# Convolved columns moved into a stage of seven-product multiplications, the SSD recurrence read by chunk from DRAM

## The chip, the cores and the metric

One core of a Trainium2 chip runs the whole kernel. TensorE (PE in the profile, with its weight loads as PEld) multiplies matrices, VectorE (DVE), ScalarE (ACT) and GpSimd (POOL) do the elementwise work, and every DMA of this kernel is issued from SyncE's queue (SP). The metric is the time of one execution on the device in microseconds (us). The kernel before took 2466.53 us, the median of three runs (2464.01 to 2472.35).

## What is computed

One layer of a hybrid recurrent decoder, on 1072 tokens in one pass: 16 learned meta tokens, 8 sample sequences of 4 tokens and a prompt of 1024 tokens. Each of the three kinds has its own recurrent state. Cut to what matters:

```python
u = x @ w_in                 # 1024 -> 10280 columns
qk_pre, v, o_pre, i_pre, f_pre, z, xbc_pre, dt_pre, gate_pre = split_cols(u, IN_SPLITS)
qk = silu(causal_dwconv(qk_pre))              # 1024 columns, convolution over 4 tokens
h  = mlstm_chunked(q, k, v, ig, lf, mstate)   # 4 heads, chunks of 128 tokens
ya = (sigmoid(o_pre) * headnorm(h)) @ w_proj_a
xbc = silu(causal_dwconv(xbc_pre))            # 3072 columns: xs 2048, B 512, C 512
y  = ssd_chunked(xs, dt, Bm, Cm, A, S) + D * xs   # 32 heads in 4 groups, chunks of 128
yb = groupRMS(y * silu(z)) @ w_proj_b
g  = sigmoid(gate_pre)
x1 = layer_norm(ALPHA * x + (g[0] * ya + g[1] * yb) @ w_out)
upc = causal_dwconv(x1 @ w_up)                # 1024 -> 5632, convolution over 3 tokens
x2 = layer_norm(ALPHA * x1 + (silu(upc_a) * upc_b) @ w_down)
```

Both recurrences carry a state from chunk to chunk. The outputs are x2 and the new states of both recurrences and of the convolutions.

## The kernel before, in words

Activations lie with channels on the 128 partitions and tokens along the row. All products are in fp32r with both operands split into a high and a low part (`split`, L156 to L159: ACT makes the high part, DVE the low one), and each product is three matmuls, high by high, high by low and low by high (`mm3`, L173 to L175). A **block** is 128 output columns of a weight matrix of 1024 rows: 8 parts of the contraction, three stretches of about 357 tokens (or 353, where the first 14 tokens are not needed), three matmuls each, so 72 matmuls. `w_in` has 72 such blocks beside v and the small gates: 8 for q and k, 8 for o, 16 for z, 16 for xs, 8 for B and C, 16 for the merge gates.

`seven` (L213 to L296) multiplies two blocks at a time with seven half-size products in place of eight: the weights of a pair and the activations are cut into halves by halves, sums of quarters are formed, and 7 products of 4 parts, two stretches of 266 and 264 tokens and three matmuls give 168 matmuls for a pair. The sums of weights are made by POOL, split by ACT and DVE, five products ahead (`AHEAD`); the results are put together by DVE, ACT and POOL in `evac`. PSUM has 8 banks (`pg` 3, `pr` 5), and `seven` uses all of them in every pair.

The stages, in order:

1. Layer norm of x, v and the small gates (to about 169 us). At its end the forms of x for `seven` are made (`make_forms`) and 2 gate blocks run in full.
2. **Early stage**, `seven` on 12 pairs of w_in: o and z. o goes to DRAM as tanh (`od`), z as silu (`zd`).
3. **mLSTM stage**: four heads of nine chunks. Each head's q and k are multiplied in full (`conv_steps`: 72 matmuls, then the copy out of PSUM, three DVE operations over 1096 elements for the taps, a tanh and three DVE operations for silu). Behind head h come 2, 1, 1 and 2 blocks of xs, B and C of SSD group 0 (`FILLS`), stored to `xsd`. The result h goes to DRAM (`hd`).
4. **SSD stage**: four groups of eight heads, nine chunks each. `begin(c)` loads the decays of a chunk (`dec`, 8 rows of 128 tokens broadcast to 128 partitions, and `E`), applies mask and exp, transposes xs and B, and multiplies by C; `end(c)` forms the output, updates the state S and adds it into `xs` in place. xs, B and C of a whole group lie in SBUF. `weave` puts between these steps the blocks of xs, B and C of the next group, and gate blocks, and `z_steps` multiplies whole rows of the previous group by z, stores `yd` and sums squares.
5. 4 more gate blocks, then proj a (8 blocks on the eight pairs of `hd`), proj b (16 blocks), w_out (8 blocks) with the layer norm, and 4 blocks of w_up in full (1310 to 1763 us).
6. `seven` on 20 pairs of w_up with the convolution over 3 tokens beside it (`act_steps`), to about 2183 us, then w_down and the last norm.

The order of instructions on each engine is made ahead of the run by a list scheduler: it takes instructions by priority (the order in which they are written, moved forward inside `tc.high_priority`), when its own estimates say that their inputs are there and a buffer of their pool is free. On the chip each engine, and the SP queue, runs its list in that order and waits where something is late. Weights are loaded 150 priority steps ahead (`WAHEAD`).

Of the kernel before, what the change touches and what calls it, by code (L numbers as in the profile page):

```python
# [1 line left out]

# [10 lines left out]
ALU = mybir.AluOpType  # L13
# [23 lines left out]
HP = [(0, 266), (266, 264)]  # L37

PLAIN = 2

# [3 lines left out]


GATES = (2, 0, 2, 2, 2, 4, 4)

FILLS = (2, 1, 1, 2)
# [8 lines left out]
def kernel(ctx, tc, I, O):  # L57
# [9 lines left out]
    rc_cm = tc.tile_pool(name="rc", bufs=1, side="right")  # L67
# [9 lines left out]
    xd = dr.tile([KD, 128, TC], F32, name="xd")  # L77
# [6 lines left out]
    zd = dr.tile([16, 128, TC], F32, name="zd")  # L84
    xsd = dr.tile([6, 128, T], F32, name="xsd")
# [117 lines left out]
    def make_forms(src, dst):  # L203
# [5 lines left out]
        V.tensor_tensor(b21, b22, b21, ALU.subtract)  # L209
# [4 lines left out]
    def seven(pairs, raws, sums, X, tmp, xforms, evac, begin=None, between=None):  # L214
# [6 lines left out]
        wf = [wp.tile([128, 2, 4, 128], F32R, tag=t, name="wf") for t in ("wl", "ws", "wh") for _ in range(2)]  # L221
# [32 lines left out]
        X = X[:, 0:4 * 266].rearrange("p (a t) -> p a t", t=266)  # L254
        for n in range(AHEAD):
            prepare(n)
        for i in range(len(pairs)):
            if begin:
                begin(i)
            for p, xf in enumerate(xforms):  # L260
# [6 lines left out]
                for j, (t0, w_) in enumerate(HP):  # L267
# [52 lines left out]
    xh = xp.tile([128, KD, CUT + 2 * HC], F32R, name="xh")  # L320
    xl = xp.tile([128, KD, CUT + 2 * HC], F32R, name="xl")
    zero = rc.tile([128, KD, 2], F32, name="zero")
    V.memset(zero, 0.0)
    split(xh[:, :, T:], xl[:, :, T:], zero)
# [10 lines left out]
    with ExitStack() as c0:  # L335
# [13 lines left out]
        def norm_in(c, t0, n):  # L349
# [21 lines left out]
            o = CUT if c == 0 else 0  # L371
            dma(xd[:, :, t0 + o - CUT:t0 + n - CUT].rearrange("k p t -> p k t"), xf[:, :, o:n])
# [186 lines left out]
    ev = tc.tile_pool(name="ev", bufs=3, side="right")  # L559
# [27 lines left out]
    def conv_steps(pool, m, cw, st_in, st_out, alloc):  # L587

        w = win_load(m)
        u = pool.tile([128, 1100], F32, tag="u", name="u", bufs=2)  # L590
        si = pool.tile([128, NB, 3], F32, tag="si", name="si", bufs=2)
        dma(si, st_in.rearrange("p (b r) -> p b r", r=3))
        G.tensor_copy(win7(u)[:, :, 0:3], si)
        G.memset(u[:, 56:59], 0.0)

        def evac(j, t0, n, ps):
            if j == 0:
                S.copy(u[:, 59:75], ps[:, 0:NMETA])
                S.copy(win7(u)[:, :, 3:7], smp(ps[:, NMETA:NA]))
                S.copy(u[:, 75:27 + n], ps[:, NA:n])  # L600
            else:
                S.copy(u[:, 27 + t0:27 + t0 + n], ps)
        for j, _ in enumerate(gemm_steps(w, NT, x_rhs, evac)):
            if j < 2:
                yield
        so = pool.tile([128, 27], F32, tag="so", name="so", bufs=2)
        G.tensor_copy(so[:, 0:3], u[:, 1096:1099])
        G.tensor_copy(so[:, 3:27].rearrange("p (b r) -> p b r", r=3), win7(u)[:, :, 4:7])
        dma(st_out, so)
        cv = pool.tile([128, 1096], F32, tag="cv", name="cv")  # L610
        S.activation(cv, u[:, 0:1096], AF.Identity, scale=cw[:, 0:1], bias=cw[:, 4:5])  # L611
        for j in range(1, 4):
            V.scalar_tensor_tensor(cv, u[:, j:j + 1096], cw[:, j:j + 1], cv, op0=ALU.mult, op1=ALU.add)  # L613
        t = u[:, 0:1096]
        S.activation(t, cv, AF.Tanh)
        dst = alloc()
# [960 lines left out]
```

## Time and profile before

| | |
|---|---|
| median of 3 runs | 2466.53 us |
| profiled execution, whole | 2476.02 us |
| its span from first to last instruction | 2474.1 us |
| PE, PEld busy | 95%, 90% of the span |
| DVE, ACT, POOL busy | 68%, 39%, 27% |
| mean granted clock of TensorE | 0.978 |
| DMA | 310.6 MB, 126 GB/s on average |

The profile is one execution. A matmul's busy time overlaps the next one's, so the pace of TensorE is read from the number of matmuls in a stretch and not from the mean length of one. A stretch's count (x...) takes in the one or two instructions that are under way at its edges. DMA share is the mean busy share of the 16 DMA engines.

### The profile page before, as it was taken

The page shows a single profiled execution, that of the slowest core. Times are in us where ns is not written, and L with a number is a line of the kernel's source. Part 1 is how long each engine was busy: PE and PEld are TensorE (multiplying, and loading weights), DVE is VectorE, ACT ScalarE, POOL GpSimd, SP SyncE. Part 2 cuts the span into 40 slices and gives each one's busy share as a digit, 9 for nine tenths or more (in the row PEclk, how much of TensorE's full clock was granted, in tenths as well). Part 3 has the DMA queues.
Part 4 walks back from the last instruction along what each step waited for, and adds up shares of the span by engine and source line. Part 5 has one row for each costly group of instructions (what it writes and reads, how often), then busy time and mean ns, then how long its engine had stood idle before and what let it go on. Part 6 is the DMA issues. An engine that isn't in the chain of part 4 may idle for free. (4 is left out here: it accounts for less than half of the span.)

```text
span 2474.1 us, 40641 instructions
## 1 busy us (share of the span) xinstructions
PE 2356.4 (95%) x15603; PEld 2233.5 (90%) x15603; DVE 1675.8 (68%) x2871; ACT 972.8 (39%) x1996; POOL 662.9 (27%) x695
## 2 busy tenths in 40 slices
PE   7989999999999999898889999999899999999996
PEld 5879999898878888797789999999899999999996
DVE  7674455678758678785746557577988888874338
ACT  6234443444345445554522112245544444441111
POOL 0034331111024233332300000033655555510004
PEclk9989999999999999999989999999999999999998
DMA  8143332544354454635646433254222222282121
GB/s 244 51 147 112 103 104 87 162 152 143 126 176 129 144 152 102 207 84 181 156 157 239 140 104 122 77 162 148 90 80 80 80 80 80 89 271 80 46 65 70
DMA packets 191122, 310.62 MB, mean 126 GB/s; under 512 B 41080, under 2 KB 131032, under 8 KB 190928
## 3 DMA queue, kind: packets, MB, share of 16 engines
q1 hardware_dynamic: 190928, 308.03, 39.8%
q8 instruction: 122, 2.00, 0.3%
q14 instruction: 72, 0.59, 0.1%
HBM read 225.39 MB, written 82.58 MB: 124 GB/s over the span
## 5 line engine op out<-in xcount | busy, mean ns | idle before, releaser
L173 PE MATMUL gps<-xh,whi 128*128 128x358 f32 (+5 forms) x1176 | 404.7, 344 | 12.6 <-ACT evt L583 6.3
L175 PE MATMUL gps<-xh,wlo 128*128 128x358 f32 (+5 forms) x1176 | 393.9, 335 | 0.0
L174 PE MATMUL gps<-xl,whi 128*128 128x358 f32 (+5 forms) x1176 | 391.5, 333 | 0.0
L158 ACT ACTIVATE whi<-wst 128x1024 fp32r<-128x1024 f32 (+1 forms) x137 | 139.5, 1019 | 433.0 <-PE gps L174 261.8
L173 PEld LDWEIGHTS gps<-xh,whi 128*128 128x128 f32 (+1 forms) x1176 | 226.6, 193 | 27.2 <-issue 9.7
L159 DVE TENSOR_TENSOR wlo<-wst,whi 128x1024 fp32r<-128x1024 f32 (+1 forms) x137 | 170.2, 1244 | 105.6 <-ACT whi L158 105.5
L174 PEld LDWEIGHTS gps<-xl,whi 128*128 128x128 f32 (+1 forms) x1176 | 226.3, 192 | 10.9 <-issue 10.3
L175 PEld LDWEIGHTS gps<-xh,wlo 128*128 128x128 f32 (+1 forms) x1176 | 226.7, 193 | 5.2 <-issue 4.7
L173 PE MATMUL gps<-ph,whi 128*128 128x352 f32 (+1 forms) x472 | 155.1, 330 | 4.8 <-ACT whi L158 1.7
L175 PE MATMUL gps<-ph,wlo 128*128 128x352 f32 (+1 forms) x472 | 154.7, 328 | 0.3 <-DVE wlo L159 0.2
L174 PE MATMUL gps<-pl,whi 128*128 128x352 f32 (+1 forms) x472 | 154.8, 328 | 0.0
L274 PE MATMUL rps<-x1h,wf 128*128 128x266 f32 (+1 forms) x480 | 137.8, 287 | 1.7 <-ACT mix L279 1.7
L275 PE MATMUL rps<-x1l,wf 128*128 128x266 f32 (+1 forms) x480 | 137.7, 287 | 0.0
L889 ACT ACTIVATE dec<-dec,tk 128x128 f32<-128x128 f32 (+1 forms) x288 | 88.4, 383 | 124.2 <-POOL dec L886 112.7
L276 PE MATMUL rps<-x1h,wf 128*128 128x266 f32 (+1 forms) x480 | 137.1, 286 | 0.0
L159 DVE TENSOR_TENSOR wf<-raw,wf 128x512 fp32r<-128x512 f32 x96 | 105.1, 1096 | 32.8 <-ACT wf L158 31.5
L1288 DVE SCALAR_TENSOR_TENSOR mix<-mix,c_fcw 128x1072 f32<-128x1072 f32 x80 | 115.6, 1445 | 6.8 <-ACT mix L1286 6.7
L613 DVE SCALAR_TENSOR_TENSOR cv<-u,c_scw,cv 128x1096 f32<-128x1096 f32 x72 | 103.1, 1432 | 17.1 <-ACT cv L611 16.7
L173 PE MATMUL gps<-ah,whi 128*128 128x352 f32 x312 | 101.0, 324 | 0.0
L175 PE MATMUL gps<-ah,wlo 128*128 128x352 f32 x312 | 100.9, 323 | 0.0
L174 PE MATMUL gps<-al,whi 128*128 128x352 f32 x312 | 100.7, 323 | 0.0
L173 PE MATMUL rps<-ph,whi 128*128 128x352 f32 (+1 forms) x296 | 96.3, 325 | 0.0
(488 smaller groups left out, 7066.1 us busy)
## 6 DMA issues: line engine op xcount, KB each, us to landing
wst<-in_win SPq DMA_DIRECT2D x48, 512.0 KB, 4.4
raw<-in_wup SPq DMA_DIRECT2D x40, 512.0 KB, 3.6
dec<-btd SPq DMA_DIRECT2D x32, 512.0 KB, 5.9
gt<-gd SPq DMA_DIRECT2D x24, 529.0 KB, 3.5
raw<-in_win SPq DMA_DIRECT2D x24, 512.0 KB, 3.4
wst<-in_wout SPq DMA_DIRECT2D x24, 512.0 KB, 3.5
fd<-mix SPq DMA_DIRECT2D x22, 528.0 KB, 2.7
raw<-fd SPq DMA_DIRECT2D x22, 528.0 KB, 4.4
```

The costliest lines, as they stand in the source:

```text
L158: S.activation(hi, src, AF.Copy)
L159: V.tensor_tensor(lo, src, hi.bitcast(F32), ALU.subtract)
L173: PE.matmul(out, ah, bh, start=start, stop=False)
L174: PE.matmul(out, ah, bl, start=False, stop=False)
L175: PE.matmul(out, al, bh, start=False, stop=stop)
L274: PE.matmul(ps, wh[:, k], a, start=new and k == 0, stop=False, **chk)
L275: PE.matmul(ps, wh[:, k], b, start=False, stop=False, **chk)
L276: PE.matmul(ps, wl[:, k], a, start=False, stop=k == 3, **chk)
L613: V.scalar_tensor_tensor(cv, u[:, j:j + 1096], cw[:, j:j + 1], cv, op0=ALU.mult, op1=ALU.add)
L889: S.activation(dec[:n, i, 0:n], dec[:n, i, 0:n], AF.Exp, bias=tk2[:n, c, g * 8 + i:g * 8 + i + 1], scale=1.0)
L1288: V.scalar_tensor_tensor(cv, u[:, j:j + 1072], fcw[:, m, j:j + 1], cv, op0=ALU.mult, op1=ALU.add)
```

## The change

**`seven` takes all convolved columns.** The early stage becomes 28 pairs: 16 pairs of q, k, xs, B and C (`conv`) and 12 of o and z (`plain`), dealt so that one or two `conv` pairs stand before each `plain` one. The halves become 536 tokens (`HX`, stretches of 268 and 268) so that all 1072 tokens are there. The results of a `conv` pair are put into `uA` and `uB`; the taps, tanh and silu (`conv_steps`) run between the products of this pair and the next, and q and k go to `qkd`, xs, B and C to `xsd`, in DRAM. The fourth form of x has no tiles of its own any more: it overwrites the second half of `xh` and `xl` (k 0 to 3) and those are restored from `xd` behind the stage. The six tiles for split weights are taken in another order of pool tags.

```diff
-GATES = (2, 0, 2, 2, 2, 4, 4)
-FILLS = (2, 1, 1, 2)
+GATES = (2, (2, 2, 1, 1), 8)
+PROJ = 6
+RAHEAD = 60
...
-        wf = [wp.tile([128, 2, 4, 128], F32R, tag=t, name="wf") for t in ("wl", "ws", "wh") for _ in range(2)]
+        wf = [wp.tile([128, 2, 4, 128], F32R, tag=t, name="wf") for t in ("ws", "ws", "wh", "wl", "wh", "wl")]
...
+        for q in range(12):
+            to = 16 * (q + 1) // 12
+            for i in range(nc_, to):
+                jobs.append(conv[2 * i:2 * i + 2])
+            nc_ = to
+            jobs.append(plain[2 * q:2 * q + 2])
...
+        def conv_steps(b, to, cw, st_out):
+            u = us[b]
...
+            S.activation(cv, u[:, 0:1096], AF.Identity, scale=cw[:, 0:1], bias=cw[:, 4:5])
+            for j in range(1, 4):
+                V.scalar_tensor_tensor(cv, u[:, j:j + 1096], cw[:, j:j + 1], cv, op0=ALU.mult, op1=ALU.add)
+                yield
+            t = u[:, 0:1096]
+            S.activation(t, cv, AF.Tanh)
+            yield
...
+            dma(to, dst)
+            yield
...
+        run(state[0])
+        for k in range(4):
+            dma(last(k), xd[k, :, HX:T])
+            split(xh[:, k, HX:T], xl[:, k, HX:T], last(k))
```

**The mLSTM stage** loads q and k of a head from `qkd`, and behind the heads come 2, 2, 1 and 1 gate blocks.

```diff
-            for _ in range(FILLS[h]):
-                fill_unit(next(fills))
+            for _ in range(GATES[1][h]):
+                run(gate_steps(next(gates)))
             if h < 3:
-                qk = qk_units(h + 1)
+                qk = qk_load(h + 1)
```

**The SSD stage** keeps no group in SBUF. Each chunk loads its xs, B and C (`xc`, 6 x 128 rows of 512 bytes) and its z (4 x 128 rows), multiplies by z, stores `yd` (4 x 128 rows) and sums squares itself. Loads of `xc` and `dec` stand two chunks ahead (`open_`), the four groups are chained, and their steps have a priority of 60 (`RAHEAD`). `dec` has 3 buffers instead of 2, `xc` 4, `z`, `E`, `tmp` 2.

```diff
+            def open_(c):
+                t0, n = CHUNKS[c]
+                xc = stile([128, 6, 128], "xc", 4)
+                dma(xc, xsd[g, :, :, t0:t0 + 128].rearrange("i p t -> p i t"))
+                dec = stile([128, 8, 128], "dec", 3)
                 dma(dec[:n, :, 0:n], btd[g * 8:(g + 1) * 8, t0:t0 + n].partition_broadcast(n))
...
+            def begin(c):
...
+                zt = stile([128, 4, 128], "z", 2)
+                dma(zt[:, :, 0:n], zd[4 * g:4 * g + 4, :, t0:t0 + n].rearrange("i p t -> p i t"))
...
+                V.tensor_tensor(x, x, tmp[:, :, 0:n], ALU.add)
+                V.tensor_tensor(x, x, zt[:, :, 0:n], ALU.mult)
+                a = CUT if c == 0 else 0
+                dma(yd[4 * g:4 * g + 4, :, t0 + a - CUT:t0 + n - CUT].rearrange("i p t -> p i t"), x[:, :, a:n])
+                sq = tmp[:, :, 0:n]
+                S.activation(sq, x, AF.Square)
+                G.tensor_tensor(sq[:, 0:2], sq[:, 0:2], sq[:, 2:4], ALU.add)
```

**Proj a begins beside the SSD.** What is woven between the steps is now 8 gate blocks and then 6 of the 8 blocks of proj a; the pairs of `hd` are loaded and split there (`hpair`). The last two blocks of proj a are queued behind the last norm of the SSD.

```diff
+        def work():
+            for q in range(GATES[2]):
+                yield from gate_steps(next(gates))
+                if 2 <= q < 6:
+                    hpair(hq, hst, q - 2)
...
+            for k in range(4, 8):
+                hpair(pm, hst, k)
+            yield from chain(*proj)
+
+        weave(chained(0, 1, 2, 3), work(), 3 * (GATES[2] + PROJ))
...
+    yp = [ypair(k, pb) for k in range(2)]
+    for s_ in proj:
+        with tc.issue_after(held[-1].ins):
+            run(s_)
```

The pools of the later stages are laid out anew (`pm` 16, `pb` 12 and `pa` 12 buffers for `pa` 20 and `pb` 20).

## Rows read from the trace of the kernel before

**Rows 1.** The page: span, and busy time with its share of the span for each engine.

```profile
span 2474.1 us, 40641 instructions
PE 2356.4 (95%) x15603; PEld 2233.5 (90%) x15603; DVE 1675.8 (68%) x2871; ACT 972.8 (39%) x1996; POOL 662.9 (27%) x695
```

**Rows 2.** Busy time of each engine by stretch, one row a stage: early stage, mLSTM, SSD with the last gate blocks, proj to w_up in full, `seven` on w_up, w_down. Columns: stretch, its length, PE, PEld, DVE, ACT, POOL busy us (instructions), granted clock, DMA share, GB/s.

```profile
176.80:425.50 248.70, 248.37 (x1989) 247.63 (x1990) 132.31 (x240) 100.23 (x225) 85.14 (x71) 0.99 0.31 101
425.50:712.00 286.50, 283.16 (x1641) 256.24 (x1640) 211.01 (x532) 119.48 (x268) 36.39 (x74) 0.99 0.46 150
712.00:1310.00 598.00, 551.11 (x3543) 491.25 (x3542) 423.10 (x647) 282.21 (x736) 186.21 (x201) 0.95 0.52 148
1310.00:1763.00 453.00, 439.18 (x2677) 433.09 (x2676) 289.09 (x417) 135.99 (x191) 69.10 (x63) 0.99 0.42 137
1763.00:2183.00 420.00, 415.63 (x3348) 414.87 (x3347) 351.01 (x482) 202.34 (x368) 238.09 (x238) 0.99 0.27 89
2183.00:2474.10 291.10, 267.79 (x1676) 265.87 (x1674) 150.92 (x295) 55.63 (x63) 34.87 (x25) 0.97 0.30 98
```

**Rows 3.** The same view for stretches in which TensorE does one kind of work and is never idle: `seven` on w_up, `seven` on w_in, blocks with stretches of 352 or 354 tokens, blocks with 358 or 356.

```profile
1800.00:2150.00 350.00, 350.00 (x2850) 350.00 (x2850) 291.32 (x409) 166.61 (x305) 205.53 (x204) 1.00 0.24 80
250.00:300.00 50.00, 50.00 (x408) 50.00 (x407) 24.80 (x48) 20.43 (x45) 16.49 (x14) 1.00 0.29 95
1350.00:1400.00 50.00, 50.00 (x309) 50.00 (x308) 26.57 (x29) 9.58 (x9) 0.00 (x0) 1.00 0.51 159
430.00:460.00 30.00, 30.00 (x184) 30.00 (x184) 16.76 (x19) 13.25 (x33) 7.68 (x15) 1.00 0.76 246
```

**Rows 4.** The same view for line L173 alone (the first of the three matmuls of a product in full blocks): the counts tell how many blocks a stretch holds. Columns: PE, PEld busy (instructions), clock, DMA share, GB/s.

```profile
425.50:712.00 286.50, 124.72 (x375) 71.02 (x376) 0.99 0.46 150
712.00:1310.00 598.00, 256.26 (x728) 142.60 (x729) 0.95 0.52 148
```

**Rows 5.** What TensorE waited for, between 145 and 425 us.

```profile
PE rps L274 <- ACT wf L158: 7.1, 1, 7.1
```

**Rows 6.** DVE by line and form: in the mLSTM and SSD stages the taps, the writing out of a convolved block (three pieces), the splitting of a block's weights and the operations of a chunk; in the early stage the splitting of weights and two of the results; in `seven` on w_up the splitting of weights.

```profile
L613 DVE SCALAR_TENSOR_TENSOR cv<-u,c_scw,cv 128x1096 f32<-128x1096 f32 x72 | 103.1, 1432 | 17.1 <-ACT cv L611 16.7
...
L618 DVE SCALAR_TENSOR_TENSOR xs<-u,cv 128x1024 f32<-128x1024 f32 x12 | 16.4, 1364 | 0.0
...
L619 DVE SCALAR_TENSOR_TENSOR xs<-u,cv 128x32 f32<-128x32 f32 x12 | 6.5, 544 | 0.0
...
L618 DVE SCALAR_TENSOR_TENSOR xs<-u,cv 128x16 f32<-128x16 f32 x12 | 4.5, 372 | 5.7 <-ACT u L615 5.6
...
L159 DVE TENSOR_TENSOR wf<-sum,wf 128x512 fp32r<-128x512 f32 x48 | 38.1, 799 | 21.1 <-ACT wf L158 20.6
L159 DVE TENSOR_TENSOR wf<-raw,wf 128x512 fp32r<-128x512 f32 x36 | 32.0, 891 | 31.9 <-ACT wf L158 30.6 <-DMA raw<-in_win 1.3
...
L654 DVE TENSOR_TENSOR e<-rps,u 128x266 f32<-128x266 f32 (+1 forms) x24 | 10.3, 433 | 6.2 <-PE rps L276 5.9
...
L159 DVE TENSOR_TENSOR wf<-raw,wf 128x512 fp32r<-128x512 f32 x52 | 64.8, 1246 | 0.0
L159 DVE TENSOR_TENSOR wf<-mix,wf 128x512 fp32r<-128x512 f32 x68 | 47.0, 691 | 41.2 <-ACT wf L158 39.4
```

**Rows 7.** The DMA queue of all loads and stores, first in the mLSTM stage (425.5 to 712 us), then in the SSD stage (712 to 1310 us). Columns: packets, MB, share of 16 engines over the stretch.

```profile
q1 hardware_dynamic: 19640, 42.58, 45.2%
...
q1 hardware_dynamic: 85840, 88.09, 51.6%
```

**Rows 8.** Busy time by stretch again, for three stretches with much DMA: the first loads and stores of x, and two of the SSD stage. The last two columns are DMA share and GB/s.

```profile
15.00:60.00 45.00, 41.34 (x192) 31.09 (x192) 33.36 (x112) 31.92 (x72) 0.00 (x0) 1.00 0.95 238
1160.00:1185.00 25.00, 23.78 (x158) 19.08 (x159) 18.53 (x32) 10.58 (x29) 12.55 (x10) 1.00 0.81 259
1200.00:1225.00 25.00, 20.89 (x163) 16.03 (x161) 19.56 (x30) 13.30 (x46) 10.60 (x10) 1.00 0.61 125
```

**Rows 9.** DMA issues: operands, queue, count, KB of each, median us from issue to landing.

```profile
dec<-btd SPq DMA_DIRECT2D x32, 512.0 KB, 5.9
...
E<-ebtd SPq DMA_DIRECT2D x64, 128.0 KB, 4.8
...
va<-vd SPq DMA_DIRECT2D x4, 1024.0 KB, 7.1
...
qp<-wind SPq DMA_DIRECT2D x4, 536.0 KB, 5.4
```

**Rows 10.** What the SP queue waited for before it issued, in the SSD stage, longest first: line of the DMA, releaser, us in total, times, longest.

```profile
SPq L584 <- ACT evt L583: 106.7, 29, 7.7
SPq L609 <- POOL so L607: 49.7, 16, 8.9
SPq L592 <- POOL u L594: 47.6, 8, 8.4
SPq L877 <- PE rps L968: 40.9, 16, 6.5
```

More of the change, by code (lines that the diff above doesn't have):

```diff
@@ new lines @@
+        sx = [(M_XS + m, xsd[m // 4, m % 4] if m < 16 else xsd[m % 4, 4 + (m - 16) // 4],
+               scw[:, m], I["scs"][m], O["sco"][m]) for m in range(24)]
+        conv = qk + sx
+        plain = [(M_O + m, od[m], None) for m in range(8)] + [(M_Z + m, zd[m], True) for m in range(16)]
+        jobs, nc_ = [], 0
+        for q in range(12):
[4 more added lines that the diff above has]
+            jobs.append(plain[2 * q:2 * q + 2])
@@ new lines, in evac, with between @@
+            S.activation(e, c, AF.Tanh, scale=0.5)
+            if z:
+                V.scalar_tensor_tensor(e, e, 1.0, c, op0=ALU.add, op1=ALU.mult)
+                dma(job[1][:, t0:t0 + n], e)
+            else:
+                a0 = max(t0, CUT)
+                dma(job[1][:, a0 - CUT:t0 + n - CUT], e[:, a0 - t0:n])
+        state = [iter(())]
+        def between(i, p):
+            if is_conv[i] and p == 2:
+                run(state[0])
+                for b in range(2):
+                    x_begin(b, jobs[i][b][3])
+                return
+            if is_conv[i] and p == 4:
+                state[0] = conv_steps(0, *jobs[i][0][1:3], jobs[i][0][4])
+            if is_conv[i] and p == 6:
+                state[0] = chain(state[0], conv_steps(1, *jobs[i][1][1:3], jobs[i][1][4]))
+            near = is_conv[i] and is_conv[i + (1 if p > 3 else -1)]
+            for _ in range(2 if near else 1):
+                next(state[0], None)
@@ L683 @@
+        run(state[0])
+        for k in range(4):
+            dma(last(k), xd[k, :, HX:T])
+            split(xh[:, k, HX:T], xl[:, k, HX:T], last(k))
     with ExitStack() as c1:
@@ L1086, with weave @@
-    for m in gates:
-        run(gate_steps(m))
-    def ptile(dt, nm, w=TC, pool=pa):
-        return pool.tile([128, PW], dt, tag="P", name=nm)[:, 0:w]
-    def pair(src):
-        f = ptile(F32, "pf")
-        dma(f, src)
-        return pair_of(f)
-    def pair_of(f, pool=pa):
+                    steps.append(lambda c=c: ahead(c))
+                steps.append(lambda c=c: end(c))
+            return steps + [norm]
+        def weave(rec, work, n):
+            done = 0
+            for k, step in enumerate(rec):
+                with tc.high_priority(RAHEAD):
+                    step()
+                to = n * (k + 1) // len(rec)
+                for _ in range(to - done):
+                    next(work, None)
+                done = to
+            run(work)
@@ L1174 @@
         gemms(unit_b, prhs(yp))
-    mpair = [pair_of(mix[k]) for k in range(8)]
+    mpair = [pair_of(mix[k], pm if k < 4 else pa) for k in range(8)]
     summed = []
```

504 lines of the change are left out of this document (237 added, 267 removed).

## The prediction

> **What bounds the kernel now.** I read the busy times first [rows 1], then the same by stage [rows 2], then the pace of TensorE where it does one thing only [rows 3]. The reader should see that PE is at 95% and that no other engine has over 68%. By stage PE is full in the early stage and in `seven` on w_up, and loses time in the SSD stage: 551.1 of 598 us busy, granted clock 0.95, so a part of that stage also ran at the lower of the clock's two levels. So the end is set by TensorE: its matmuls, and what it loses beside the recurrences.
>
> Pace [rows 3], counts less 1.5 for the instructions at the edges: `seven` with about 265 tokens needs 350 us / 2848 = 122.9 ns a matmul, on w_in 123.0; full blocks 162.6 ns with 353 tokens and 164.4 ns with 357. The pace falls with the tokens, by (164.4 - 122.9) / 92 = 0.45 ns a token, so a product of fewer columns does cost less, and the slower pace per column eats part of it. A pair of blocks in full is 144 x 164.4 ns = 23.7 us; as seven products 168 x 122.9 ns = 20.65 us.
>
> **The change, part by part.** The sum is made on the profiled span of 2474.1 us.
>
> *Early stage.* With 268 tokens a matmul needs 122.9 + 3 x 0.45 = 124.2 ns, a pair 20.87 us, 28 pairs 584.4 us, against 248.7 now [rows 2]: **+335.7**. Taking 32 blocks out of the other stages removes 32 x 72 x 164.4 ns = 378.8 us, so the products alone give some 43 us.
>
> This holds if DVE keeps up. A `conv` pair costs it [rows 6] six tap operations x 1.432 = 8.6 us, two writings out x (1.364 + 0.372 + 0.544) = 4.6, seven splits of weights x 0.835 (70.1 / 84) to 0.93 (111.8 / 120) = 5.8 to 6.5, eight results x 0.43 = 3.4 and small pieces, about 0.6: 23 to 23.7 us, more than the 20.9 of PE. A `plain` pair costs 132.3 / 12 = 11 us [rows 2]. Over the stage that is 16 x 23.3 + 12 x 11 = 505 of 584 us (86%); over two `conv` pairs and a `plain` one 57.6 of 62.6 (92%). In `seven` on w_up DVE stands at 291 of 350 us (83%) and PE has no gap [rows 3]. Weights are split five products (15 us) ahead, and the taps may run into the next pair, so I expect the bursts to be absorbed but for a few us. Bounds: 0, and 3.5 x 16 = 56 us if nothing is absorbed (2.4 us of excess a pair, and splits at the 1.246 us of the slowest row would add 2.2 more: the middle). Restoring `xh` adds four splits behind the last product; they lie beside the first head's small matmuls, else cost some 4 us. Together I take **+6**.
>
> The stage now begins with 7.1 us in which PE waits for the first split weights [rows 5], because the tile was still held by the gate blocks. The new order of tags frees it earlier. Bounds 0 and -7, taken **-5**: what is late then is the load of the weights, which reuse the tiles in which the forms of x are made.
>
> *mLSTM stage.* It holds 375 / 24 = 15.6 blocks [rows 4], 185 us; the recurrence's own part is 286.5 - 185 = 101.6 us, 98.3 of it busy. After: six gate blocks x 72 x 162.6 ns = 70.3, plus the own part: 169 to 172 us if the blocks still fill each wait. They fill less, two behind a head or one (11.7 us) where there were three or four. At the start of a head `va` and `qp` need 7.1 and 5.4 us to land [rows 9], and both have a single buffer. Uncovered in every head that is some 9 x 4 = 36 us, so the bounds are 168 and 214. I take 178, near the row: **-108.5**. The q and k loads replace weight loads and cost nothing while DMA stays at half share [rows 2].
>
> *SSD stage.* It holds 728 / 24 = 30.3 blocks [rows 4], 358 us, and its own part is 240 us, 193 of it busy. After: eight gate blocks and six of proj a, 164 us. PE alone therefore asks for 357 us (no wait left) to 404 us (the same waits as now).
>
> The new term is DMA. From the two stages [rows 7] a price follows for packets and bytes: 45.2% of 286.5 is 129.5 us for 19,640 packets and 42.58 MB; 51.6% of 598 is 308.6 us for 85,840 and 88.09. Solved: 0.90 us a thousand packets and 2.63 us a MB, all 16 engines together. A full chunk moves rows of 512 bytes: `xc` 768, `dec` 1024, `E` 512, `z` 512, `yd` 512, together 3328 packets and 1.70 MB, where it moved 1536 of that kind. 32 full chunks, four short ones (10,700 packets, 2.9 MB), the sample states in and out (16.8 MB), 14 weights (7.3), gates and `hd` (12), and the 4-byte packets of the semaphores: about 136,000 packets and 94.5 MB, so 123 + 248 = **371 us** of all 16 engines. In the stretch from 15 to 60 us [rows 8] a share of 0.95 was held for 45 us, so a stage of 390 us is possible, and it lies within what PE asks for. DVE (5.6 us a chunk, some 280 with the rest) and ACT stay below. I take 390: **-208**. Bounds: 357, if PE alone decides, and 464 (below).
>
> The Trainium skill, "DMA: Bandwidth & Descriptors", section Specifications, gives 512 bytes as the least size that moves at line rate. The price from the rows disagrees: 0.90 + 0.512 x 2.63 = 2.25 us a thousand packets of 512 bytes, 40% of which goes with the packet and not with its bytes. By the rule only the bytes would count, 94.5 x 2.63 = 248 us, DMA would be no limit, and the third rival would come out.
>
> *Proj a.* Six of eight blocks leave the stage after 1310 us: **-70.3** (they are counted above). The last two wait in order behind the last norm of the SSD; their 23 us cover the loads of the first pairs of y. Smaller pools further on can hold an act of w_down until the last product on w_up is done, 2 us at most; costed at nothing.
>
> *Sum.* 2474.1 + 335.7 + 6 - 5 - 108.5 - 208 - 70.3 = 2424 us. Outside the span lie 1.9 us (2476.02 - 2474.1), so 2426. The profiled execution is 1.0038 times the median of the three runs, so the median should be **2417 us**, 2% less.
>
> **The rivals.**
>
> *DMA starves the SSD stage (slower).* All transfers go through one SP queue, which waits in order. A store of `yd` waits for the multiplication by z, and a load of `dec` or `E` for a buffer; everything written behind them waits too, the weights of proj a among them. SP already waits 106.7 us at the stores of gates and 40.9 us at `dec` [rows 10]. Against it: loads stand two chunks ahead. In the SSD stage the share was 0.81 and 0.61 in two stretches that move the most [rows 8]. At 0.80 the stage takes 371 / 0.80 = 464 us, 74 more than forecast: 2490. It decides from the point where the share falls below 371 / 440 = 0.84, since 440 us is the length at which the gain is gone.
>
> *DVE is the bound of the early stage.* Nothing of the excess of `conv` pairs is absorbed: 56 us in place of 6: 2466, no change. For it speaks the 92% in a group of three; against it the stage on w_up.
>
> *The recurrences fill themselves (faster).* DMA costs only its bytes and the waits go: SSD 357, mLSTM 169, start -7, no loss in DVE: 2424 - 33 - 9 - 2 - 6 = 2374, median 2367. For it: the waits of today's SSD come partly from convolutions in the queues of DVE and ACT, which leave. Against it: PE has fewer blocks to put into each gap.
>
> *Too little filler in the mLSTM stage.* 214 us in place of 178: 2453.
>
> That seven products save nothing is ruled out by the pace [rows 3].
>
> **How the numbers follow.** Forecast 0.50 (2417; alone 2390 to 2445); DMA 0.18 (2490); DVE 0.09 (2466); self-filling 0.15 (2367); mLSTM 0.08 (2453). About 0.3%, 7 us, can be told from no change. Faster: 0.48 + 0.15 + 0.06 + 0.02 (from DVE) = 0.71. Same: 0.02 + 0.03 + 0.04 + 0.02 = 0.11. Slower: 0.15 from DMA and 0.03 from DVE = 0.18. The range takes in both outer cases: 2360 to 2490.
>
> **What would show it.** Right: the early stage at about 168 matmuls in 20.9 us with no PE gaps, ending near 760 us; mLSTM near 180 us; SSD near 390 us with a DMA share over 0.9. Wrong: gaps of PE in the early stage that end on DVE; a SSD stage over 440 us in which weights or `dec` arrive late; or one with a DMA share well under 0.9 that is short all the same, which would mean that the price of packets was wrong.

## The result and the profile after

The changed kernel takes 2502.76 us (median of 4 runs, 2499.45 to 2504.03) against 2469.44 before (4 runs): 1.0131 times, 95% interval 1.0101 to 1.0162. It is 1.3% slower, clear of the noise; 2417 us and a gain were forecast, and the time lies above the range too. The profiled execution took 2504.03 us.

The page of the changed kernel, span and busy time of each engine, to be read against [rows 1]:

```profile
span 2502.4 us, 42291 instructions
PE 2339.1 (93%) x16059; PEld 2209.5 (88%) x16059; DVE 1772.9 (71%) x3021; ACT 995.0 (40%) x2075; POOL 813.6 (33%) x823
```

TensorE does have less to do, 2339 us in place of 2356, but the span is 28 us longer: 163 us without work where there were 118. The stages say where. Busy time by stretch of the changed kernel, in the order and columns of [rows 2]: early, mLSTM, SSD, proj to w_up in full, `seven` on w_up, w_down.

```profile
174.20:771.00 596.80, 587.21 (x4704) 584.58 (x4705) 482.20 (x706) 266.80 (x530) 278.05 (x295) 0.99 0.32 102
771.00:968.00 197.00, 184.86 (x1026) 158.33 (x1024) 131.50 (x444) 65.05 (x171) 9.31 (x14) 0.97 0.66 215
968.00:1402.00 434.00, 359.62 (x2325) 293.48 (x2325) 277.42 (x451) 203.23 (x620) 177.85 (x176) 0.91 0.81 213
1402.00:1785.00 383.00, 372.21 (x2256) 366.27 (x2257) 262.52 (x387) 126.75 (x182) 61.22 (x56) 0.99 0.42 139
1785.00:2206.00 421.00, 416.07 (x3356) 415.86 (x3355) 351.85 (x485) 203.60 (x367) 239.17 (x237) 0.99 0.28 90
2206.00:2502.40 296.40, 268.82 (x1659) 267.06 (x1657) 147.48 (x292) 52.45 (x61) 32.50 (x25) 0.96 0.28 94
```

Only the third row is far from its forecast of 390 us. In its 434 us TensorE works 359.6 and stands for 74.4, at a granted clock of 0.91; before, it stood for 46.9 us of a longer stage, at 0.95. How many blocks the mLSTM and the SSD stage hold is told by the first matmul of a product alone, as in [rows 4]:

```profile
771.00:968.00 197.00, 62.08 (x180) 35.02 (x180) 0.97 0.66 215
968.00:1402.00 434.00, 107.19 (x298) 59.65 (x298) 0.91 0.81 213
```

180 / 24 = 7.5 blocks and 298 / 24 = 12.4: 20 together, as forecast, with one and a half of them a stage earlier. At 11.7 us a block the mLSTM stage has an own part of 197 - 88 = 109 us (forecast 178 - 70 = 108), the SSD stage one of 434 - 145 = 289 us (forecast 390 - 164 = 226, before 240). That one number, 63 us, is most of the miss of 78.

The DMA queue in the same two stages, columns as in [rows 7]:

```profile
q1 hardware_dynamic: 20096, 42.08, 65.5%
q1 hardware_dynamic: 133109, 92.18, 81.0%
```

133,109 packets and 92.2 MB, against 136,000 and 94.5 in the forecast; 81% of 434 is 352 us of all engines, against 371. So the transfers are those that were counted, a little cheaper, and the share isn't 0.95. Within the stage, two stretches of 50 us (columns as above):

```profile
1000.00:1050.00 50.00, 43.08 (x326) 35.84 (x326) 38.43 (x53) 28.53 (x90) 27.19 (x26) 0.97 0.82 202
1200.00:1250.00 50.00, 32.81 (x210) 22.91 (x210) 33.20 (x49) 23.11 (x69) 23.91 (x23) 0.81 0.89 229
```

Where the share is 0.89, TensorE works 33 of 50 us and its clock is down to 0.81. What TensorE waited for in the SSD stage (line of the matmul, releaser, us in total, times, longest):

```profile
PE rps L1055 <- POOL tmp L1045: 36.8, 16, 5.5
PE rps L970 <- DMA s<-in_s0T: 7.9, 4, 6.3
PE rps L931 <- ACT acol L309: 7.4, 4, 4.0
PE rps L931 <- DMA xc<-xsd: 5.6, 6, 2.1
```

Half of the waiting is put down to L1045, a POOL addition of squares at the end of a chunk, the last link of a chunk's chain; only 14 us to transfers directly. And the SP queue waits ahead of its issues, columns as in [rows 10]:

```profile
SPq L1042 <- DVE xc L1040: 30.9, 16, 7.7
SPq L1000 <- DVE s L999: 25.2, 13, 8.2
SPq L919 <- DVE tmps L987: 23.0, 4, 6.9
SPq L901 <- DMA yd<-xc: 22.8, 12, 3.6
```

L1042 is the store of y, L1000 that of the sample states, L919 and L901 the loads of E and of a chunk's columns. Before a run there were thus four suspects: the transfers themselves, POOL in the chain, the order of SP's queue, and too little filler where it is wanted.

### The profile page after: what moved, and what is told of

Same layout as the page of the kernel before. It is cut to its first block, busy times and chain, and to the rows that moved or that the text cites. A ratio compares the mean times of both kernels' runs of the same rounds, so it can differ in the third digit from the quotient of the medians.

```text
span 2502.4 us, 42291 instructions
## 1 busy us (share of the span) xinstructions
PE 2339.1 (93%) x16059; PEld 2209.5 (88%) x16059; DVE 1772.9 (71%) x3021; ACT 995.0 (40%) x2075; POOL 813.6 (33%) x823
## 4 chain that ended last, share of the span: by engine, by line
PE 43%; DMA 7%; DVE 6%; POOL 2%; ACT 2%; issue 2%; SPq 0%; POOLq 0%; DVEq 0%; ACTq 0%
PE gps L180 5%; PE gps L182 5%; PE gps L181 5%; PE rps L284 4%; PE rps L282 4%; PE rps L283 4%; PE rps L180 3%; PE rps L182 3%; PE rps L181 3%; DMA dec<-btd 2%; PE gps L282 2%; PE gps L284 2%; PE gps L283 2%; DMA xc<-xsd 1%; PE rps L1010 1%
## 5 line engine op out<-in xcount | busy, mean ns | idle before, releaser
L282 PE MATMUL rps<-xh,wf 128*128 128x268 f32 x672 | 195.0, 290 | 14.7 <-ACT wf L165 7.6
L284 PE MATMUL rps<-xh,wf 128*128 128x268 f32 x672 | 193.8, 289 | 2.3 <-DVE wf L166 2.3
L283 PE MATMUL rps<-xl,wf 128*128 128x268 f32 x672 | 193.3, 288 | 0.0
L166 DVE TENSOR_TENSOR wf<-raw,wf 128x512 fp32r<-128x512 f32 x144 | 145.3, 1014 | 15.7 <-ACT wf L165 15.6
L180 PE MATMUL gps<-xh,whi 128*128 128x352 f32 (+3 forms) x408 | 141.2, 346 | 3.7 <-ACT whi L165 1.8
L282 PEld LDWEIGHTS rps<-xh,wf 128*128 128x128 f32 x672 | 128.1, 191 | 17.0 <-ACT X L289 8.9
L182 PE MATMUL gps<-xh,wlo 128*128 128x352 f32 (+3 forms) x408 | 139.5, 343 | 0.0
L181 PE MATMUL gps<-xl,whi 128*128 128x352 f32 (+3 forms) x408 | 138.8, 340 | 0.0
L284 PE MATMUL rps<-x1h,wf 128*128 128x266 f32 x480 | 137.5, 287 | 0.0
L282 PE MATMUL rps<-x1h,wf 128*128 128x266 f32 x480 | 137.5, 286 | 0.0
L283 PE MATMUL rps<-x1l,wf 128*128 128x266 f32 x480 | 137.2, 286 | 0.0
L284 PEld LDWEIGHTS rps<-xh,wf 128*128 128x128 f32 x672 | 127.8, 190 | 2.6 <-DVE wf L166 2.6
L283 PEld LDWEIGHTS rps<-xl,wf 128*128 128x128 f32 x672 | 128.3, 191 | 0.0
L181 PEld LDWEIGHTS gps<-pl,whi 128*128 128x128 f32 x568 | 109.7, 193 | 8.0 <-issue 4.3
```

Of the source, the lines that this page charges most:

```text
L166: V.tensor_tensor(lo, src, hi.bitcast(F32), ALU.subtract)
L180: PE.matmul(out, ah, bh, start=start, stop=False)
L181: PE.matmul(out, ah, bl, start=False, stop=False)
L182: PE.matmul(out, al, bh, start=False, stop=stop)
L282: PE.matmul(ps, wh[:, k], a, start=new and k == 0, stop=False, **chk)
L283: PE.matmul(ps, wh[:, k], b, start=False, stop=False, **chk)
```

## The experiments

The SSD stage runs here from the first transposition of a chunk to the last norm, its DMA time is the share times the length, and TensorE's idle time is the length less its busy time. All but the timed ones are single executions. One kernel (the four edits, below) timed six times gave 2436.9 to 2453.5 us, and its stage measured 375.7 and 380.8 us in two profiles, so a total says nothing below about 15 us and a stage little below 5 to 8.

| run | total us | SSD stage us | DMA us (share) | TensorE idle us |
|---|---|---|---|---|
| changed kernel | 2502.8 | 434.2 | 353 (0.81) | 74 |
| e2 without the loads of E | 2482.6 | 409.3 | 313 (0.77) | 56 |
| e3 no POOL addition | 2494.7 | 426.1 | 353 (0.83) | 54 |
| e5 rows by chunk | 2510.1 | 429.6 | 336 (0.78) | 66 |
| e8 pairs read directly | 2497.8 | 434.4 | 353 (0.81) | 71 |
| e9 = e8, z read twice | 2523.5 | 458.9 | 390 (0.85) | 87 |
| e12 two blocks more | 2505.8 | 451.1 | 356 (0.79) | 59 |
| e13 btd by chunk | 2487.6 | 418.6 | 336 (0.80) | 61 |
| e10 = e2 + e3 + e8 | 2472.3 | 396.2 | 306 (0.77) | 47 |
| e14 = e10 + e13 | 2440.8 | 375.7 | 293 (0.78) | 30 |
| kernel before | 2469.4 | 573.6 | 301 (0.52) | 47 |
| e18 before, btd by chunk | 2444.7 | 543.1 | 281 (0.52) | 28 |
| e19 = e18, E from dec | 2452.8 | 550.6 | 239 (0.43) | 33 |

**Do the transfers matter at all?** First, more of them: a copy of every chunk's silu(z) from DRAM to DRAM.

```diff
+                dma(zz[9 * g + c, :, :, 0:n], zd[4 * g:4 * g + 4, :, t0:t0 + n])
```

> The changed kernel, and every chunk's z is also copied from DRAM to a DRAM tile that nobody reads: 512 more packets a chunk, about 17,400 and 8.8 MB in all, 16 + 23 = 39 us of all 16 DMA engines by the price of 0.90 us a thousand packets and 2.63 us a MB; no engine waits for them. DMA theory (the SSD stage's 434 us are its 351 us of DMA at a share of 0.81): the stage grows by 39 / 0.81 = 48 us, the kernel to about 2550 us. Order theory (what costs is the waiting in order on POOL and PE, 37 us at the sums of squares) and filler theory (too few matmuls beside the recurrence): the stage stays within 8 us and the share of DMA rises instead.

2651.1 us, the SSD stage 493 us and the mLSTM stage 258 in place of 197. This was a bad instrument: the copies depend on nothing but z, the first of them were issued in the early stage already, at 481 us, and they slowed the mLSTM stage, which reads no z. So it is no price of what it added in the SSD stage. Next, fewer: E is worked out by ScalarE from the rows of dec before the mask (the staging buffer and the eviction tiles shrink to make room).

```diff
-                if c < 7:
-                    load_E(c + 2)
+                if c:
+                    E = st["E", c] = stile([128, 4, 128], "E", 3)
+                    for j in range(2):
+                        S.activation(E[j * 64:j * 64 + 64], dec[j * 64:j * 64 + 64, j:8:2, :], AF.Exp)
```

> The changed kernel without the loads of E, but for the first chunk of a group: ACT takes exp of the rows of dec that are in SBUF anyway (two operations a chunk, some 1.2 us). 16,400 packets and 8.4 MB less, 15 + 22 = 37 us of DMA. E has 3 buffers instead of 2; to make room evt has 3 instead of 4 and hst is loaded in thirds. DMA theory: the SSD stage shortens by 37 / 0.81 = 45 us to about 390, the kernel to about 2458 us. Order theory: within 10 us of the changed kernel, as the sums still wait for POOL. Filler theory: within 10 us, or longer by what ACT adds.

The queue and the stretch of the SSD stage in this run:

```profile
q1 hardware_dynamic: 116972, 83.53, 76.1%
...
969.50:1378.80 409.30, 353.18 (x2290) 284.26 (x2291) 278.61 (x458) 241.38 (x689) 183.10 (x176) 0.91 0.77 205
```

40 us less DMA time took 25 us off the stage, though ScalarE's work rose by 38 us. Had the DMA engines set it at a fixed share, their share would have stayed and the stage would have lost 40 / 0.81 = 49; the share fell. Part of the 25 us is not a gain either. The first matmul of a product in full blocks, first in the changed kernel and then in this run, tells how many blocks lie in the stage:

```profile
968.20:1402.40 434.20, 107.42 (x299) 59.84 (x299) 0.91 0.81 213
969.50:1378.80 409.30, 103.22 (x286) 55.46 (x286) 0.91 0.77 205
```

At 24 a block, half a block (6 us) of filler lies outside the stage here, so some 19 us are left, about what the total lost (20). The transfers are part of the cause, not all of it.

**Order and chain.** Taken out one by one: POOL's addition in the sum of squares (four small products in place of two), and SP's waiting for the store of y (issued from ScalarE's queue).

```diff
-                G.tensor_tensor(sq[:, 0:2], sq[:, 0:2], sq[:, 2:4], ALU.add)
...
-                for i in range(2):
+                for i in range(4):
```

> The changed kernel without POOL's addition of squares: four small matmuls a chunk sum them in place of two, so PE waits for ACT's squares and no longer for POOL, which stands behind the mask that waits for dec. Order theory: most of the 37 us that PE waits there go, the SSD stage comes to 400 to 410 us. DMA theory: PE waits elsewhere for the same loads; the stage stays within 8 us.

> The changed kernel with the stores of yd issued from ACT's queue behind the square, which waits for the same product, and no longer from SP's. The DMA work is the same. If it is SP's waiting in order (31 us at yd, and what stands behind it) that holds the share of DMA at 0.81, the share rises to 0.88 and the SSD stage falls to about 400 us. If it is the DMA engines' own throughput and the depth of the buffers, the stage stays within 8 us.

Without POOL's addition the stage falls by 8 us only, at the edge of what can be told, and TensorE's longest wait ends on the operation before it, ScalarE's squaring:

```profile
PE rps L1054 <- ACT tmp L1044: 15.1, 12, 3.4
```

So the 36.8 us at POOL stood mostly for the lateness of the whole chunk. The store of y on the other queue: 428.2 us, share 0.81 as before, and 3 of these 6 us are a third of a block that lies outside the stage (292 first matmuls for 299). SP now stood at the next thing of the same kind, the load into the buffer that the store has to leave:

```profile
SPq L901 <- DMA yd<-xc: 53.4, 20, 5.6
```

So the store alone isn't what held the queue; its waiting in order at everything else was still there.

**Which property of the transfers, and the filler.** Five runs follow. The first lays out the convolved columns and z by chunk in DRAM, so that a chunk is read in rows of 3072 and 2048 bytes:

```diff
-    xsd = dr.tile([4, 6, 128, T], F32, name="xsd")
+    xsd = dr.tile([4, 9, 128, 6, 128], F32, name="xsd")
...
-                dma(xc, xsd[g, :, :, t0:t0 + 128].rearrange("i p t -> p i t"))
+                dma(xc, xsd[g, c])
```

> The stored convolved columns and silu(z) are laid out by chunk, so that a chunk of the recurrences is read as 128 rows of 3072 B and 128 rows of 2048 B instead of 768 and 512 rows of 512 B; the short rows move to the stores of the early stage. 36.9 thousand packets fewer in the SSD stage, same bytes: by 0.90 us per thousand 33 us less DMA time there (353 to about 320). Theory 'the DMA queue holds the stage': the stage of 434 us falls by what the run without the E loads gave per us of DMA time (25 of 40), so by 18 to 25 us, and the early stage of 597 us does not grow by more than 3. Theory 'the filler is missing' (projection a waits for its pairs): the stage falls by under 8 us. Theory 'latency of each load in its chain': what counts is the number of loads in a row, which is the same: under 8 us as well.

34,000 packets fewer gave 17 us of DMA time, not 33, and the stage 4.6 us; the early stage, which now stores in short rows, grew by 12. A loss. The second and third read the pairs of proj a without a staging buffer, and add to that a load that nobody waits for:

```diff
-        for h in (slice(0, TC // 2), slice(TC // 2, TC)):
-            f = st()
-            dma(f, hd[k, :, h])
-            split(hi[:, h], lo[:, h], f)
+        f = lo.bitcast(F32)
+        dma(f, hd[k])
+        split(hi, lo, f)
...
+                dma(stile([128, 4, 128], "zz")[:, :, 0:n], zd[4 * g:4 * g + 4, :, t0:t0 + n].rearrange("i p t -> p i t"))
```

> The eight pairs of the projection are read straight into the tile of their low halves and split in place: no staging buffer, so no load waits for the split of the one before. Theory 'missing filler': the stretch of 1210 to 1260 us, where 21 of the filler's matmuls ran against some 50 in 25 us elsewhere, fills up; TensorE's idle time in the SSD stage (74 us) falls by 15 to 25 and so does the stage (434 to 410 to 420). Theory 'the DMA queue holds the stage': under 5 us.

> The kernel with the pairs read directly, and beside it each chunk's silu(z) is read a second time into a tile that nobody reads (18.1 thousand packets, 9.3 MB more; output unchanged): by the prices 41 us more DMA time in the SSD stage. Against the run with the pairs read directly: theory 'the DMA queue holds the stage' plus 25 to 41 us; theories 'missing filler' and 'latency of each load': plus 0 to 8 us.

The stretch of the SSD stage, first in the run with the pairs read directly:

```profile
966.80:1401.20 434.40, 363.40 (x2329) 295.35 (x2330) 275.85 (x443) 201.95 (x610) 184.12 (x176) 0.90 0.81 213
```

and with z read twice:

```profile
967.50:1426.40 458.90, 371.82 (x2333) 301.82 (x2334) 278.02 (x445) 204.12 (x611) 178.30 (x176) 0.88 0.85 222
```

The staging of the pairs isn't it: nothing moved. The load that nobody reads costs 24.5 us for 37 us of DMA time, and TensorE stands 16 us longer. The time from issue to landing (last number, median us) tells something about how, first with the pairs read directly:

```profile
dec<-btd SPq DMA_DIRECT2D x31, 512.0 KB, 6.8
xc<-xsd SPq DMA_DIRECT2D x34, 384.0 KB, 5.4
E<-ebtd SPq DMA_DIRECT2D x64, 128.0 KB, 5.1
...
yd<-xc SPq DMA_DIRECT2D x32, 256.0 KB, 4.1
```

and with z read twice:

```profile
dec<-btd SPq DMA_DIRECT2D x31, 512.0 KB, 6.2
xc<-xsd SPq DMA_DIRECT2D x34, 384.0 KB, 5.2
E<-ebtd SPq DMA_DIRECT2D x64, 128.0 KB, 4.8
...
yd<-xc SPq DMA_DIRECT2D x32, 256.0 KB, 6.8
```

The chunk's loads dec, xc and E did not get longer (z took 4.9 us in place of 4.5); the store of y did. The 36 extra loads also hold SP's queue while they are issued, 24.5 us in the sum of their durations. So the run shows that more transfers cost time in this stage, but not whether the price is paid at the DMA engines or in SP's queue.

Whether there is room for filler is asked by two more blocks of proj a beside the recurrences, and whether more loads in flight help by a fifth buffer for a chunk's columns:

```diff
-PROJ = 6
+PROJ = 8
```

> All eight products of the first projection are filler beside the recurrences instead of six: two blocks more, some 162 matmuls, which take about 24 us each behind the stage. Theory 'transfers set the SSD stage': the stage of 434 us grows only by the two blocks' own transfers, 2 to 8 us, since TensorE has 74 us without work in it; the stretch behind it falls from 382 to about 335, and the total by 39 to 45 us. Theory 'TensorE sets the stage, its waits are bubbles that filler can't use': the stage grows by 40 to 50 us and the total stays within 5 us.

> The pairs of the projection read directly, and with the room so won a fifth buffer for a chunk's six columns (xc); the eviction tiles go from four to three to make the rest of the room. Against the run with the pairs read directly (SSD stage 434): theory 'the loads can't be issued far enough ahead' (SP's loads of xc waited 21 us for the store out of the buffer four chunks before): the stage falls by 10 to 20 us and the share of the DMA engines rises above 0.83. Theory 'the DMA engines' rate' and theory 'TensorE's own work': under 5 us.

The SSD stage with all eight blocks of proj a:

```profile
965.90:1417.00 451.10, 392.35 (x2455) 313.30 (x2456) 286.05 (x461) 204.97 (x620) 178.29 (x176) 0.92 0.79 209
```

Only 128 of TensorE's instructions came into the stage by this, 1.75 blocks, and the stage grew by 17 us, where they need 21 at the 162.6 ns of full blocks [rows 3]. The stretch behind it loses just 12 us: the first pairs of y have no cover there now (one wait of 6.2 us for their split). The total is within 5 us, as the second theory has it: TensorE's idle time here is hardly usable by filler. The fifth buffer gave 4 us of the stage against the run with the pairs read directly, at a share of 0.84 and with half a block (6 us) fewer in the stage; its total was 2505.3. That is no gain.

Another order of the tiles for w_down's activations was tried beside these:

> The twelve tiles of pa come earlier and those of pb later in the list that the pairs of the activations take. Theory: the wait of 5.2 us of the first product on w_down for whi goes because the tiles that its activations stand in are free; w_down falls from 296.4 to about 290, everything before it unchanged, total minus 5 to 7 us. Rival: the wait is ScalarE's order (the split of the weight stands behind activations), then nothing changes.

The wait went from 5.2 to 1.9 us and w_down from 296.4 to 293.4; the total was 2507.8, so 3 us are not to be seen in it.

**The same bytes in fewer packets.** Each chunk's dec, 1024 rows of 512 bytes, is laid out by chunk, so that it is read as 128 rows of 4096:

```diff
-    btd = dr.tile([32, T], F32, name="btd")
+    btd = dr.tile([4, 9, 8, 128], F32, name="btd")
...
+                    dma(dec.rearrange("p h t -> p (h t)"),
+                        btd[g, c].rearrange("h t -> (h t)").partition_broadcast(128))
```

> The changed kernel with btd laid out by chunk, so that a chunk's dec is read as 128 rows of 4096 B instead of 1024 rows of 512 B: 28.7 thousand packets fewer in the SSD stage, the same bytes, and nothing else moves (btd is written once, in 8 transfers instead of 1). By the price of the layout run (17 us for 34 thousand packets) 14 us less DMA time, by the 0.90 us per thousand of the prediction 26. By the slope of the runs without E and with silu(z) twice (0.63 and 0.69 us per us of DMA time) the stage falls by 9 to 17 us, to 417 to 425. If only the number of loads in a row counts: under 4 us.

The stage is 418.6 us, minus 15.6 for 17 us less DMA time. What POOL (the mask, the first reader of dec) waited for dec in the SSD stage, first in the changed kernel and then with this layout:

```profile
POOL dec L908 <- DMA dec<-btd: 53.2, 23, 6.1
```

```profile
POOL dec L914 <- DMA dec<-btd: 32.1, 16, 4.7
```

In the trace the median time from the start of the issue of a full chunk's dec to the start of its mask (32 chunks, issues and masks paired in their order) went from 7.42 to 6.43 us, by 24 us in the sum of all chunks. So this load stands in the chunk's chain, and its own length counts. Then the edits were put together:

> Three edits together on the changed kernel: E worked out on ScalarE from dec instead of read (40 us less DMA time), the pairs read directly, the sum of squares by four small products instead of a POOL addition. If what they gave alone (21, 5 and 9 us of the total) adds up: 2468, no slower than before the change within 0.5%. If they removed the same waits: 2478 to 2482.

> The three edits together (E from dec, pairs read directly, sum of squares by four products; 2472) and the layout of btd by chunk. If the DMA time is still part of what sets the stage (396 us, share 0.77): minus 8 to 15, total 2457 to 2464, faster than before the change. If it no longer is: minus 0 to 4.

> The same four edits, and y is stored from ScalarE's queue instead of SyncE's. Alone that gave 6 us of the stage and 2 of the total. Expected against the four edits: minus 0 to 6.

> The four edits and seven products of the first projection beside the recurrences instead of six. The run with eight put 1.75 blocks more inside the SSD stage for 17 us and took 12 us off the stretch behind it. Theory 'TensorE has free time only in part': the total stays within 4 us of the four edits. Theory 'with less DMA time the bubbles are usable': minus 5 to 12.

Three edits add up nearly in full (2472.3 for 2468 expected), and the layout of btd on top gives more than expected: 2440.8. The stretch of its SSD stage:

```profile
965.40:1341.10 375.70, 345.40 (x2453) 286.82 (x2454) 271.59 (x443) 239.19 (x673) 155.63 (x140) 0.96 0.78 224
```

TensorE stands for 30 us in place of 74, its clock is back at 0.96, and the share of the DMA engines is still 0.78: the stage has become shorter than the 390 forecast at a share that was never near 0.95. The store of y from ScalarE's queue now costs 30 us of the stage (2474.6 in total) where 0 to 6 gained were expected; TensorE's wait for the squaring on ScalarE, whose queue now also holds the stores, is 15.3 us in place of 3.6. A seventh block of proj a gave 2452.4, no gain. The version with four edits was then timed, and the layout of btd put into the kernel before, by the same lines:

> The kernel of the four edits again (E from dec, pairs read directly, sum of squares by four products, btd by chunk), timed in rounds against the kernel before. From its single run 2440.8: 2437 to 2447, ratio to before 0.986 to 0.991.

> The kernel before, with btd laid out by chunk and nothing else: the same 28.7 thousand short packets fewer in its SSD stage, whose share of the DMA engines is 0.525 instead of 0.81. Theory 'transfers cost where the share is near full': the stage of 574 us falls by 0 to 4. Theory 'each dec load stands in the chain of its chunk and gets shorter': it falls as the changed kernel's did, by 12 to 16.

The four edits: 2445.57 us (6 runs), 0.9911 times the kernel before, 0.9885 to 0.9937, so 0.9% faster, and at the upper end of what was expected. The second was the surprise: the kernel before with this one edit takes 2444.67 us (4 runs), 0.9914 times, 0.9883 to 0.9944, where 0 to 4 us less, or 12 to 16, were expected. Its SSD stage, first as it was in the kernel before (queue, stretch, POOL's wait for dec):

```profile
q1 hardware_dynamic: 83739, 84.99, 52.1%
...
707.00:1280.60 573.60, 526.71 (x3395) 466.53 (x3394) 412.78 (x636) 275.15 (x733) 186.21 (x201) 0.95 0.52 149
...
POOL dec L886 <- DMA dec<-btd: 102.9, 26, 10.0
```

and with btd by chunk:

```profile
q1 hardware_dynamic: 55056, 84.95, 51.2%
...
700.90:1244.00 543.10, 515.41 (x3396) 458.36 (x3394) 416.24 (x636) 275.08 (x732) 190.11 (x201) 0.97 0.52 158
...
POOL dec L892 <- DMA dec<-btd: 79.2, 19, 8.9
```

The same number of TensorE instructions in 30.5 us less, 19 of them idle time, with the DMA engines half free before and after. A rate that is near its limit can't explain that; a load in the chunk's chain can. From issue to mask a dec now takes 4.74 us (median) in place of 6.09, 40 us less in the sum of the 32 chunks. The size is less sure than the direction: the two profiles are from the slow end of one kernel's runs (2476.0 us) and the fast end of the other's (2437.9), and the medians differ by 22 us only.

Last, E from dec in this kernel too:

> The kernel before with btd laid out by chunk and E worked out on ScalarE from dec instead of read: the two edits that gave the changed kernel 16 and 25 us of its SSD stage when made alone. If E's load is in the chain of a chunk here too, the stage of 543 us (with btd by chunk alone) falls by another 8 to 20 and the total from 2445 to 2425 to 2437, faster than the changed kernel with its four edits. If the two exponentials and their wait for dec cost as much as the load: 2440 to 2455.

```profile
703.30:1253.90 550.60, 517.56 (x3395) 461.48 (x3394) 410.86 (x636) 314.79 (x796) 188.03 (x201) 0.97 0.43 140
```

2452.75 us (4 runs), 0.9928 times the kernel before (0.9900 to 0.9955): nothing gained on the layout alone, the second of the two outcomes written down. 41 us of DMA time less gained nothing at a share of 0.52; but the exponentials now stand ahead of the mask (6.35 us from issue to mask), so the run doesn't price the transfers alone. The same edit took 25 us off the changed kernel's stage, at 0.81.

## Why the prediction was wrong

**What bounds the kernel, and the pace.** Right: a product of 268 tokens needs what [rows 3] said. A stretch of the early stage:

```profile
250.00:300.00 50.00, 50.00 (x408) 50.00 (x407) 39.25 (x56) 23.48 (x49) 20.88 (x23) 1.00 0.34 110
```

50 us / 406.5 = 123.0 ns a matmul, for 124.2 forecast. The early stage took 596.8 us for 590 forecast. The excess of DVE in `conv` pairs was absorbed (DVE 81% busy; 2.3 us of TensorE's waiting end there), and the gaps end on ScalarE instead, in the results X and once at the start:

```profile
PE rps L282 <- ACT wf L165: 7.9, 2, 7.6
PE rps L282 <- ACT X L289: 7.0, 8, 2.6
PE rps L284 <- DVE wf L166: 2.3, 1, 2.3
```

The first row holds the start's wait, which the forecast let go for -5: it didn't go. The rival that DVE bounds the early stage is out.

**mLSTM stage.** Right: own part 109 us for 108, at two filler blocks a head. It is 19 us longer than forecast because the weave began a block and a half earlier, which the SSD stage got back.

**SSD stage.** This is the step that failed: "a share of 0.95 was held for 45 us [rows 8], so a stage of 390 us is possible, and it lies within what PE asks for." The stage was priced as the larger of two rates, the transfers at the best share seen and TensorE at no extra wait, with the two lying beside each other in full. It came out at 434 us, the transfers at 81% and TensorE at 83% busy, neither at its limit. Two things of the steps around it held: the count of packets and bytes, and the price, too high by some 3% (0.90 x 133.1 + 2.63 x 92.2 = 362 us for 352), though its part for the packet was too high by more (last section). The stretch at 0.95 held bulk loads and stores of x; in no profile of the changed kernel's variants did the SSD stage hold a share over 0.85, and the shortest of them (376 us) ran at 0.78. What the runs put in place of the step:

- A chunk waits for its own loads, and their duration is part of its chain. Shown by the layout of btd: the same bytes, the same work, shorter loads, and 15.6 us off this stage in one profile each, 30.5 off the one of the kernel before (22 us by the medians), where the DMA engines were half free.
- More transfers cost on top. Shown by the load that nobody reads (plus 24.5 us for 37 us of DMA time) and, from the other side, by E (minus 25 for 40, 6 of them filler that lies outside); where the share was 0.52, taking E's loads out gained nothing. How they cost isn't shown: beside the unread load dec, xc and E took no longer to land, and it takes time on SP's queue too. E's edit also moves work to ScalarE.
- TensorE's idle time in this stage is hardly usable: 21 us of filler more made it 17 us longer, and a seventh block beside the four edits gained nothing either.

**The rivals.** "DMA starves the SSD stage" had the nearest place, and its condition was met (share 0.81, below 0.84). Its total, 2490 for 2503, came near by luck in part: it had the stage at 464 us in place of 434, 30 too many, and the other stages 34 too short. Of its mechanism, a single SP queue that waits in order, only the store of y was tested: off that queue, it changed the stage by 6 us and the share not at all. The waiting at the loads behind it was left, and no run takes it out. That the recurrences fill themselves is ruled out. The Trainium skill, "DMA: Bandwidth & Descriptors", section Specifications, gives 512 bytes as the least size that moves at line rate. The trace doesn't agree: with the bytes unchanged (92.1 MB both), 28.6 thousand packets fewer, rows of 512 bytes read as rows of 4096, saved 17 us of DMA time.

**The rest of the sum.** Proj a to w_up 382 us for 382.7 and `seven` on w_up as before. w_down took 5.3 us more, nearly all in one wait at its start, where "2 us at most; costed at nothing" stood:

```profile
PE gps L180 <- ACT whi L165: 5.2, 1, 5.2
```

In all: SSD +44, mLSTM +19, early +6, w_down +5, the start and the rest +4, together 2502 for 2424.

**What stays open.** How the 63 us divide between the length of the single loads and the price of more transfers, and whether that price is paid at the DMA engines or in SP's queue. SP issues during 191 of the 434 us (the durations of its DMA instructions in the trace) and waits in order for nearly all the rest. Its issuing alone doesn't set the stage: the store moved off it took 37 us of issuing for 6 us of the stage, and the layout of btd in the kernel before 6 us of issuing for 30. What its waiting in order costs stays open. The four edits took 58 and 53 us off the stage in two profiles (3 of them filler that lies outside), about the sum of what each gave alone (25, 8, 0 and 16), so most of it is accounted for by edits but not split between the causes. The lower granted clock is in these times too and wasn't measured apart. Why the store of y on ScalarE's queue hurts only beside the other edits wasn't followed further.

## What to carry to other kernels

Where a stage reads its operands by small steps, don't price it as the largest of its engines' rates: list the loads in one step's chain, with their time from issue to first reader, and see which of them the next engine stands waiting for. A stage can stall with the DMA engines half free: here TensorE stood for 47 of 574 us at a share of 0.52, and for 74 of 434 at 0.81. Before a large restructuring, try the layout in DRAM of the most frequent load: here a few lines on btd in the kernel before gave as much as the whole change with four repairs. And a wait named in the profile can be the last link only, as the 36.8 us at POOL were: remove it, and see whether the time goes or moves to the link before.

## What was not expected of the hardware

- Reading rows of 512 bytes as rows of 4096 saved 0.60 us of all 16 engines' time per thousand packets fewer in the changed kernel (17.1 us for 28.6 thousand) and 0.7 in the kernel before, and 0.49 where rows of 2 and 3 KB took its place; the price solved from two stages was 0.90.
- The granted clock followed TensorE's idle time and not the DMA share: 0.91 with 74 us of idle time in the SSD stage, 0.96 with 30 us at nearly the same share, and 0.81 in the 50 us in which TensorE was busy for 33. The matmuls that run at the lower of the two levels are part of the 434 us; how large a part, no run shows.
- Moving the store of y to ScalarE's queue was worth 6 us of the stage at most in one version and cost 30 in another.
